# A streaming-encoder trunk in fp32: when the eighth block's weights are loaded and scaled, and in what order keys and queries are split

## The chip, the cores and the metric

The kernel runs on one core of one Trainium2 chip. The metric is the device time of a run in microseconds, the median of several runs.

## The reference

The input x has 256 rows of 2048. Layer A: RMSNorm, one projection to queries, keys, values and gate (4096 wide each, 32 heads of 128), attention with a learned bias by relative distance, product with SiLU(gate), output projection, residual. Layer B: keys and values of a shared stream, forget gates from it, queries and gate of its own projection, causal attention with accumulated decays, gate, output projection, residual. A last RMSNorm follows. Everything is float32.

```python
# layer A
q, k, v, g = split(rms_norm(x, a_norm) @ a_w_in, 4)
x = x + (chunked_relbias_attention(q, k, v, rel_bias) * silu(g)) @ a_w_out
# layer B
h_kv = rms_norm(x, kv_norm)
k, v = split(h_kv @ kv_w, 2)
cum = cumsum(log_sigmoid(h_kv @ f_w + f_b))
q, g = split(rms_norm(x, b_norm) @ b_w_in, 2)
x = x + (forgetting_attention(q, k, v, cum) * silu(g)) @ b_w_out
out = rms_norm(x, final_norm)
```

## The kernel before

Every float32 product is made of three matmuls. A factor is split into a high part (ScalarE, ACT, copies it to the rounded type fp32r) and a low part (VectorE, DVE, subtracts the high part from the original); high x high, high x low and low x high are summed by TensorE (PE), in `mm3` for the projections and `dot3` for the rest.

The heads go in 16 pairs. Each pair has two **units** of 512 weight columns: in layer A `aqk` (queries and keys) and `avg` (values and gate), in layer B `bqg` (queries and gate) and `bkv` (keys and values). A unit consumes its 2048 input rows in blocks of 256 rows; pairs after the first have seven such blocks in each unit. `Feed` brings a block in: SyncE (SP) sends the load of 512 KB into one of three raw buffers, ACT and DVE split it into one of four split buffers, PE takes 12 matmuls from it. In layer B the split also multiplies by the norm's gain. `Feed` keeps up to four blocks split ahead.

The eighth block of both units of a pair is done together in the third step of the pair's first unit, as a **quad**: its four 128-row by 512-column weight tiles (two of each unit) and four row-by-column tiles of x are multiplied in seven products instead of eight, after Strassen's scheme in Winograd's form. `Quads.products` does this from sums of x made once (`sums`) and differences of the weights. `load_quad` loads the next pair's two weight blocks into one kept buffer `raw`, in layer B scales them by the gain, and makes the first differences; `quad` splits the four operands when their turn comes in the feed. `behind` is an ordering trick: ACT copies one column of a block that is ready into the destination, so that what follows cannot be placed or sent earlier than that block's split.

The attention of a pair runs beside the projections of the following pair, as a generator (`side_a`, `side_b`, both around `attention`) that `drive` advances at the steps named in a table. Its stages: transposing queries and keys by DVE and 16 small DMAs from GpSimd (`turn`, `sums` or `b_sums` is the target), splitting keys (`wideh`, `widel`) and queries (`q1h`, `q1l`), the scores (`s1p`, `s0p`), softmax, transposing the probabilities (`sgY` to `sgZ`), splitting them (`wideh`, `widel` again), the product with the values (`op`), the gate. `B1_STEPS` says after which steps of layer B's first unit the stages of the pair before it are issued; `hooks` are calls after a step. The previous pair but one (`old`) is finished in steps 0 and 1.

The order of the program is that of issue by these tables; the tile framework's scheduler then sets the order on each engine, which runs its instructions strictly in that order. Each engine waits for others by semaphores.

Of the kernel before, what the change touches and what calls it, by code (L numbers as in the profile page):

```python
# [10 lines left out]
F32R = mybir.dt.float32r  # L11
BF16 = mybir.dt.bfloat16
AF = mybir.ActivationFunctionType
# [3 lines left out]
P = 128  # L17
S = 256
NT = S // P
# [13 lines left out]
HG = 2  # L33
NG = H // HG
GC = HG * DH
UN = 512
KB = 2
SQ = 32
# [16 lines left out]
QK7_STEPS = {0: 1, 5: 1, 6: 2}  # L55
PV7_STEPS = {0: 1}
QUAD = 7
QUAD_STEP = 3
B1_STEPS = {2: 1, 4: 1, 5: 2}
B2_STEPS = {0: 1}  # L60


def r32(ap):
    return ap.bitcast(F32)
# [3 lines left out]
def trunk(ctx, tc, x, x_t, gains, a_w_in, a_rel, a_w_out, kv_w, f_w, f_b, b_w_in, b_w_out, final_norm, out):  # L68
    nc = tc.nc
    pe, act, dve, pool, sp = nc.tensor, nc.scalar, nc.vector, nc.gpsimd, nc.sync  # L70
# [4 lines left out]
    att = ctx.enter_context(tc.tile_pool(name="att", bufs=1))  # L75
# [104 lines left out]
    class Feed:  # L180
# [68 lines left out]
                    break  # L249

        def load_quad(self, layer, g):

            q = quads[layer]
            raw, t = q.raw, q.t
            for r in range(2):
                self.behind(raw[:, r, :, :1], -1)
                sp.dma_start(out=raw[:, r], in_=q.w(r, g))
                for j in range(KB) if q.g0 else ():
                    act.activation(raw[:, r, j], raw[:, r, j], AF.Copy,  # L259
                                   scale=gain[:, q.g0[r] + QUAD * KB + j:][:, :1])  # L260
            dve.tensor_sub(t[:, 0], raw[:, 1], raw[:, :, 0])  # L261
            dve.tensor_sub(raw[:, 1, 0], raw[:, 1, 1], t[:, 0, 0])
# [66 lines left out]
    feed = Feed(todo)  # L329
# [28 lines left out]
    def rest(u):  # L358

        for b in range(u.nk // KB - u.left, u.nk // KB):  # L360
            u.step(b)
            yield u.acc
# [36 lines left out]
    def evac_scaled(acc, c0, c1, rs, dst):  # L399
        for t in range(NT):  # L400
            act.activation(dst[:, t], acc[t][:, c0:c1], AF.Copy, scale=rs[:, t:t + 1])

    def split(srcs, tag, place=None):

        n, nt = len(srcs), srcs[0].shape[1]
        hi = att.tile([P, n, nt * P], F32R, name=f"{tag}h", tag=f"{tag}h")
        lo = att.tile([P, n, nt * P], F32R, name=f"{tag}l", tag=f"{tag}l")
        if place is not None:
            feed.behind(hi[:, :, :1], place)
        for k, src in enumerate(srcs):  # L410
            h, l = (v[:, k].rearrange("p (t i u) -> p t i u", t=nt, u=SQ) for v in (hi, lo))
            act.activation(h, src, AF.Copy)
            dve.tensor_sub(l, src, r32(h))
        return hi, lo

    def dot3(out_, a, b, start=True, stop=True):
        pe.matmul(out_, a[0], b[0], start=start, stop=False)
# [3 lines left out]
    def attention(g, biases, qk, vg, half, ocat, queues=(pool,) * NQ, line=(None, None), home=None):  # L421
# [3 lines left out]
        bias1, bias0 = biases()  # L425
        qkT = z.rearrange("p i (t c) u -> p c t i u", t=NT)
        yield
        kh, kl = split([qkT[:, HG + i] for i in range(HG)], "wide", line[0])
        qh, ql = split([qkT[:, i, 1:] for i in range(HG)], "q1", line[0])
        q0 = att.tile([P, HG, P], F32, name="q0", tag="oT")  # L430
        if line[0] is not None:
            feed.behind(q0[:, :, :1], line[0])
# [48 lines left out]
        hi = ocat.hi[h0 // BIG][:, h0 % BIG:h0 % BIG + HG, :]  # L481
        lo = ocat.lo[h0 // BIG][:, h0 % BIG:h0 % BIG + HG, :]
# [15 lines left out]
    def rows(n, name):  # L498
        return att.tile([P, NT, n], F32, name=name, tag="R")
# [193 lines left out]
    rs, prev, qa = [], None, quads["a"]  # L693
    for g in range(NG):
        accs = {}
        if g:
            accs["quad"] = True
            first, second = (Unit(xT, next(order)) for _ in range(2))
            accs["qk"] = drive(rest(first), prev, PV7_STEPS,
                               {QUAD_STEP - 1: lambda: qa.products(first, second, (rsA, [(t, UN) for t in range(NT)]))})  # L700
            vg = rest(second)
        else:
            first, second = woven_units()
            rsA, halfA = rs
            accs["qk"], vg = first.acc, rest(second)
        old, prev = prev, side_a(g, accs)
        advance(prev)
        accs["vg"] = drive(vg, prev, QK7_STEPS, {0: lambda: g + 1 < NG and feed.load_quad("a", g + 1)}, old, 1)
        if not g:
            qa.sums_of_x()  # L710
        close_vg(accs)
# [150 lines left out]
    def open_b(accs):  # L862
        qk, qg = rows(UN, "qk"), accs["qg"]
        if "quad" in accs:
            qb.first_half(qk[:, :, :GC], qg, 0, rsB)
            qg = qb.whole_sums(qg, 0, GC)
        else:
            evac_scaled(qg, 0, GC, rsB, qk[:, :, :GC])
        accs["q"] = qk, gate_from(qg, GC, halfB)

    old = prev = None
    fg = forget()
    for g in range(NG):
        accs = {}
        first, second = (Unit(x1T, next(order)) for _ in range(2))
        hooks = {}
        if g:
            accs["quad"] = True
            hooks[QUAD_STEP - 1] = lambda: qb.products(first, second, (rsB, [(i, GC) for i in range(2 * NT)]))
        accs["qg"] = drive(rest(first), prev, B1_STEPS, hooks, old, 1)  # L880
        hooks = {0: lambda: g + 1 < NG and feed.load_quad("b", g + 1), 2: lambda: open_b(accs)}
        accs["kv"] = drive(rest(second), prev if g else fg, B2_STEPS if g else {1: 1, 2: 1, 4: 1, 6: 1}, hooks)
        if not g:
            qb.sums_of_x()
        old, prev = prev, side_b(g, accs)
        advance(prev)
# [95 lines left out]
```

## Time and profile before

| | |
|---|---|
| runs | 1879.86, 1882.55, 1884.58 us; median 1882.55 |
| profiled execution | 1873.8 us, of it a span of 1872.1 |
| mean granted clock of TensorE | 0.994 |
| DMA | 396.37 MB, mean 212 GB/s |

The profile is of one execution, and it was a faster one than the three timed. In its rows L232 is line 232 of the kernel, PE is TensorE's matmuls and PEld its weight loads, an arrow `out<-in` names the tiles. Layer A's pairs run from about 11 to 705 us, its output projection to 915, layer B's pairs from there to 1651, its output projection to the end.

### The profile page before, as it was taken

To read this page: it belongs to the slowest core of one execution; us is meant where nothing else is said; L and a number is where in the kernel's file an instruction comes from. 1 tells how busy PE (TensorE), PEld (TensorE's weight loads), DVE (VectorE), ACT (ScalarE), POOL (GpSimd) and SP (SyncE) were. 2 spreads that over 40 slices of the span, in tenths; PEclk is the share of its full clock that TensorE was granted. 3 is DMA by queue.
4 is the path that set the end of the run, shared out by engine and by line. 5 is a ranking of instruction groups with operands and counts; after the bars stand their busy time and mean duration, and the time that the engine had idled before them with its cause. 6 is when DMAs were issued, how large, how long until landed. Compare 5 with 4: busy or idle time off the path is not lost.

```text
span 1872.1 us, 25978 instructions
## 1 busy us (share of the span) xinstructions
PE 1840.7 (98%) x8297; PEld 1514.4 (81%) x8297; DVE 1424.1 (76%) x2094; ACT 1184.7 (63%) x2233; POOL 522.2 (28%) x1071
## 2 busy tenths in 40 slices
PE   9999999999999999999999999999999999999998
PEld 7888888888888888888887878878778887878886
DVE  7877878888788877555678878888888878886554
ACT  6665656666566656444567777777777777775443
POOL 1222222232222223221023333333323333333000
PEclk9999999999999999999999999999999999999999
DMA  8666666666666666776656656666666665667664
GB/s 283 214 212 212 225 215 220 213 219 213 210 213 213 210 210 207 240 234 224 209 176 204 206 198 211 210 208 210 208 207 202 216 204 194 210 220 222 206 202 158
DMA packets 143144, 396.37 MB, mean 212 GB/s; under 512 B 31104, under 2 KB 37536, under 8 KB 142880
## 3 DMA queue, kind: packets, MB, share of 16 engines
q1 hardware_dynamic: 106960, 354.25, 57.7%
q0 software_dynamic: 32256, 37.29, 6.7%
q10 hardware_dynamic: 3792, 3.17, 0.6%
q8 instruction: 66, 1.08, 0.2%
q14 instruction: 70, 0.57, 0.1%
HBM read 351.05 MB, written 4.23 MB: 190 GB/s over the span
## 4 chain that ended last, share of the span: by engine, by line
PE 30%; DMA 12%; DVE 10%; ACT 9%; issue 3%; POOL 0%; ACTq 0%; DVEq 0%
PE bo_acc L176 9%; PE ao_acc L176 8%; PE bqg_acc L176 5%; DMA b_quad<-in_kv_w 5%; DMA bqg_raw<-in_b_w_in 3%; DVE bqg_lo L233 3%; PE bkv_acc L176 3%; DMA bkv_raw<-in_kv_w 3%; ACT bkv_hi L232 3%; ACT sg L451 1%; DVE bkv_lo L233 1%; PE avg_acc L176 1%; PE aqk_acc L176 1%; ACT b_quad L259 1%; DVE b_quad L261 1%
## 5 line engine op out<-in xcount | busy, mean ns | idle before, releaser
L395 POOL DMA_DIRECT2D sgZ<-sgY x512 | 251.4, 498 | 529.2 <-PE bkv_acc L176 299.9
L236 ACT ACTIVATE avg_hi<-avg_raw 128x1024 fp32r<-128x1024 f32 x112 | 118.7, 1060 | 138.3 <-DMA avg_raw<-in_a_w_in 76.7
L237 DVE TENSOR_TENSOR avg_lo<-avg_raw,avg_hi 128x1024 fp32r<-128x1024 f32 x112 | 136.2, 1217 | 87.8 <-ACT avg_hi L236 87.6
L232 ACT ACTIVATE bqg_hi<-bqg_raw,gain 128x512 fp32r<-128x512 f32 x226 | 150.1, 713 | 60.3 <-DMA bqg_raw<-in_b_w_in 49.0
L233 DVE SCALAR_TENSOR_TENSOR bqg_lo<-bqg_raw,gain,bqg_hi 128x512 fp32r<-128x512 f32 x226 | 163.6, 773 | 26.5 <-ACT bqg_hi L232 26.3
L233 DVE SCALAR_TENSOR_TENSOR bkv_lo<-bkv_raw,gain,bkv_hi 128x512 fp32r<-128x512 f32 x226 | 159.0, 744 | 22.8 <-ACT bkv_hi L232 22.6
L176 PE MATMUL bqg_acc<-bqg_hi,x1Th 128*128 128x512 f32 x452 | 174.7, 398 | 0.0
L176 PE MATMUL bqg_acc<-bqg_lo,x1Th 128*128 128x512 f32 x452 | 174.4, 397 | 0.0
L176 PE MATMUL bqg_acc<-bqg_hi,x1Tl 128*128 128x512 f32 x452 | 173.1, 394 | 0.0
L176 PE MATMUL aqk_acc<-aqk_hi,xTh 128*128 128x512 f32 x452 | 173.0, 394 | 0.0
L176 PE MATMUL avg_acc<-avg_hi,xTh 128*128 128x512 f32 x452 | 172.3, 393 | 0.0
L176 PE MATMUL aqk_acc<-aqk_lo,xTh 128*128 128x512 f32 x452 | 170.9, 390 | 0.4 <-DVE aqk_lo L237 0.4
L176 PE MATMUL aqk_acc<-aqk_hi,xTl 128*128 128x512 f32 x452 | 171.0, 390 | 0.0
L176 PE MATMUL avg_acc<-avg_hi,xTl 128*128 128x512 f32 x452 | 170.9, 390 | 0.0
L176 PE MATMUL bkv_acc<-bkv_hi,x1Th 128*128 128x512 f32 x452 | 170.8, 389 | 0.0
L176 PE MATMUL bkv_acc<-bkv_lo,x1Th 128*128 128x512 f32 x452 | 170.8, 389 | 0.0
L176 PE MATMUL bkv_acc<-bkv_hi,x1Tl 128*128 128x512 f32 x452 | 170.7, 389 | 0.0
L176 PE MATMUL avg_acc<-avg_lo,xTh 128*128 128x512 f32 x452 | 170.6, 389 | 0.0
L395 POOL DMA_DIRECT2D b_sums<-b_quad x256 | 125.8, 499 | 151.2 <-issue 86.6
L232 ACT ACTIVATE bkv_hi<-bkv_raw,gain 128x512 fp32r<-128x512 f32 x226 | 150.4, 712 | 18.1 <-DMA bkv_raw<-in_kv_w 7.5
L395 POOL DMA_DIRECT2D sums<-quad x192 | 94.7, 499 | 219.4 <-PE op L475 84.5
L237 DVE TENSOR_TENSOR aqk_lo<-aqk_raw,aqk_hi 128x1024 fp32r<-128x1024 f32 x110 | 132.2, 1221 | 26.6 <-ACT aqk_hi L236 25.8
(317 smaller groups left out, 4372.9 us busy)
## 6 DMA issues: line engine op xcount, KB each, us to landing
bqg_raw<-in_b_w_in SPq DMA_DIRECT2D x113, 512.0 KB, 4.3
bkv_raw<-in_kv_w SPq DMA_DIRECT2D x113, 512.0 KB, 3.6
avg_raw<-in_a_w_in SPq DMA_DIRECT2D x112, 512.0 KB, 4.7
aqk_raw<-in_a_w_in SPq DMA_DIRECT2D x110, 512.0 KB, 4.1
ao_raw<-in_a_w_out SPq DMA_DIRECT2D x64, 512.0 KB, 4.2
bo_raw<-in_b_w_out SPq DMA_DIRECT2D x64, 512.0 KB, 4.2
sgZ<-sgY POOLq DMA_DIRECT2D x512, 40.0 KB, 4.4
quad<-in_a_w_in SPq DMA_DIRECT2D x32, 512.0 KB, 5.8
```

The source lines that it names most:

```text
L176: pe.matmul(acc[t], x[:, t * P:(t + 1) * P], w, start=t not in begun, stop=k == nk - 1 and i == 2)
L232: act.activation(hi[:, j], raw[:, j], AF.Copy, scale=gk)
L233: dve.scalar_tensor_tensor(lo[:, j], raw[:, j], gk, r32(hi[:, j]), op0=OP.mult, op1=OP.subtract)
L236: act.activation(hi[:, j], raw[:, j], AF.Copy)
L237: dve.tensor_sub(lo[:, j], raw[:, j], r32(hi[:, j]))
L259: act.activation(raw[:, r, j], raw[:, r, j], AF.Copy, scale=gain[:, q.g0[r] + QUAD * KB + j:][:, :1])
L261: dve.tensor_sub(t[:, 0], raw[:, 1], raw[:, :, 0])
L395: queues[j].dma_start(out=r32(z)[j * SQ:(j + 1) * SQ, i], in_=y[i * SQ:(i + 1) * SQ, j])
L451: act.activation(s_[:, i], s_[:, i], AF.Exp, bias=nm[:, t, i:i + 1], accum_out=sm[:, t, i:i + 1])
```

## The change

It has three parts.

1. `load_quad` is cut in two. The loads stay in it and are now called after step 5 of a pair's first unit (`LOAD_STEP`) in both layers; before, all of it was called after step 0 of the second unit. (In layer A's first pair they are called between the units.)
2. The scalings (layer B alone) and the first differences become `differ`. Layer A calls it after step 0 of the second unit, as before; layer B after step 3.
3. `split_pairs` splits several groups together, head by head: keys of head 0, queries of head 0, keys of head 1, queries of head 1, instead of both heads' keys and then both heads' queries. In layer B the stage is issued one step sooner (`B1_STEPS`: 3 in place of 4).

```diff
-B1_STEPS = {2: 1, 4: 1, 5: 2}
+LOAD_STEP = 5
+B1_STEPS = {2: 1, 3: 1, 5: 2}
...
         def load_quad(self, layer, g):
+            q = quads[layer]
+            for r in range(2):
+                self.behind(q.raw[:, r, :, :1], -1)
+                sp.dma_start(out=q.raw[:, r], in_=q.w(r, g))
+
+        def differ(self, layer):
             q = quads[layer]
             raw, t = q.raw, q.t
             for r in range(2):
-                self.behind(raw[:, r, :, :1], -1)
-                sp.dma_start(out=raw[:, r], in_=q.w(r, g))
                 for j in range(KB) if q.g0 else ():
                     act.activation(raw[:, r, j], raw[:, r, j], AF.Copy,
                                    scale=gain[:, q.g0[r] + QUAD * KB + j:][:, :1])
...
+    def split_pairs(many, place=None):
+        out = []
+        for srcs, tag in many:
+            nt = srcs[0].shape[1]
+            out.append([att.tile([P, len(srcs), nt * P], F32R, name=f"{tag}{x}", tag=f"{tag}{x}") for x in "hl"])
+            if place is not None:
+                feed.behind(out[-1][0][:, :, :1], place)
+        for k in range(len(many[0][0])):
+            for (srcs, _), (hi, lo) in zip(many, out):
+                h, l = (v[:, k].rearrange("p (t i u) -> p t i u", t=srcs[k].shape[1], u=SQ) for v in (hi, lo))
+                act.activation(h, srcs[k], AF.Copy)
+                dve.tensor_sub(l, srcs[k], r32(h))
+        return out
...
-        kh, kl = split([qkT[:, HG + i] for i in range(HG)], "wide", line[0])
-        qh, ql = split([qkT[:, i, 1:] for i in range(HG)], "q1", line[0])
+        (kh, kl), (qh, ql) = split_pairs([([qkT[:, HG + i] for i in range(HG)], "wide"),
+                                          ([qkT[:, i, 1:] for i in range(HG)], "q1")], line[0])
...
             accs["qk"] = drive(rest(first), prev, PV7_STEPS,
-                               {QUAD_STEP - 1: lambda: qa.products(...)})
+                               {QUAD_STEP - 1: lambda: qa.products(...),
+                                LOAD_STEP: lambda: g + 1 < NG and feed.load_quad("a", g + 1)})
...
-        accs["vg"] = drive(vg, prev, QK7_STEPS, {0: lambda: g + 1 < NG and feed.load_quad("a", g + 1)}, old, 1)
+        accs["vg"] = drive(vg, prev, QK7_STEPS, {0: lambda: g + 1 < NG and feed.differ("a")}, old, 1)
...
+        hooks[LOAD_STEP] = lambda: more and feed.load_quad("b", g + 1)
         accs["qg"] = drive(rest(first), prev, B1_STEPS, hooks, old, 1)
-        hooks = {0: lambda: g + 1 < NG and feed.load_quad("b", g + 1), 2: lambda: open_b(accs)}
+        hooks = {2: lambda: open_b(accs), 3: lambda: more and feed.differ("b")}
```

What the scheduler makes of it in layer B, in one pair. In the names below `bqg_hi`, `bkv_hi` are split blocks, `b_quad_8492` the quad's raw buffer, `b_quad_8493` its differences, `b_comb` the quad products' sums. First place, the second unit: the loads on SP's queue, from the third `kv` load on. Before:

```order
L197 DMA bkv_raw_13408<-in_kv_w 128x1024
L197 DMA bkv_raw_13428<-in_kv_w 128x1024
L197 DMA bkv_raw_13465<-in_kv_w 128x1024
L834 DMA cb<-cumd 128x512
L197 DMA bkv_raw_13506<-in_kv_w 128x1024
L197 DMA bkv_raw_13526<-in_kv_w 128x1024
L257 DMA b_quad_8492<-in_b_w_in 128x1024
L257 DMA b_quad_8492<-in_kv_w 128x1024
L197 DMA bqg_raw_13582<-in_b_w_in 128x1024
```

After:

```order
L198 DMA bkv_raw_13408<-in_kv_w 128x1024
L198 DMA bkv_raw_13445<-in_kv_w 128x1024
L198 DMA bkv_raw_13465<-in_kv_w 128x1024
L256 DMA b_quad_8492<-in_b_w_in 128x1024
L256 DMA b_quad_8492<-in_kv_w 128x1024
L198 DMA bkv_raw_13510<-in_kv_w 128x1024
L198 DMA bkv_raw_13530<-in_kv_w 128x1024
L846 DMA cb<-cumd 128x512
L198 DMA bqg_raw_13576<-in_b_w_in 128x1024
```

The two quad loads moved from behind the seventh `kv` load to behind the fifth; the load of the decays `cb` moved from behind the fifth to behind the seventh.

Then ACT at the same place: the ordering copies of the quad loads (`b_quad_8492<-bkv_hi`), the scalings and the last `kv` blocks. Before, from the gate's scaling to the gate of the next pair:

```order
L462 ACTIVATE sg<-gs,csc 128x128 x4
L280 ACTIVATE b_quad_8492<-bkv_hi_13520 128x2 x2
L232 ACTIVATE bkv_hi_13576<-bkv_raw_13465,gain 128x512 x2
L841 ACTIVATE d_13729<-cb,cum 128x128
L232 ACTIVATE bkv_hi_13596<-bkv_raw_13506,gain 128x512 x2
L842 ACTIVATE cb<-cb,cum 128x256
L841 ACTIVATE d_13729<-cb,cum 128x128
L842 ACTIVATE cb<-cb,cum 128x256
L232 ACTIVATE bkv_hi_13626<-bkv_raw_13526,gain 128x512
L259 ACTIVATE b_quad_8492<-b_quad_8492,gain 128x512 x4
L505 ACTIVATE gs<-b_comb,half_b 128x256 x2
```

After, from the third `kv` block on:

```order
L233 ACTIVATE bkv_hi_13504<-bkv_raw_13408,gain 128x512
L285 ACTIVATE b_quad_8492<-bkv_hi_13459 128x2 x2
L233 ACTIVATE bkv_hi_13504<-bkv_raw_13408,gain 128x512
L461 ACTIVATE sg,sm<-sg,nm 128x256 x2
L461 ACTIVATE sg,sm<-sg,nm 128x128 x2
L233 ACTIVATE bkv_hi_13524<-bkv_raw_13445,gain 128x512 x2
L472 ACTIVATE sg<-gs,csc 128x128 x4
L233 ACTIVATE bkv_hi_13570<-bkv_raw_13465,gain 128x512 x2
L264 ACTIVATE b_quad_8492<-b_quad_8492,gain 128x512 x2
L233 ACTIVATE bkv_hi_13590<-bkv_raw_13510,gain 128x512 x2
L264 ACTIVATE b_quad_8492<-b_quad_8492,gain 128x512 x2
L233 ACTIVATE bkv_hi_13620<-bkv_raw_13530,gain 128x512
```

The copies moved ahead of the softmax (`sg`), and the four scalings, which stood together behind the first half of the last block, stand two and two ahead of it; the four decays' instructions (`d`, `cb`) moved behind the last `kv` block, past the end of these rows.

Second place, ACT at the split of keys and queries. Before:

```order
L232 ACTIVATE bkv_hi_13422<-bkv_raw_13374,gain 128x512 x2
L627 ACTIVATE b_comb<-b_comb,rstd_b 128x256 x2
L280 ACTIVATE wideh<-bkv_hi_13422 128x2
L280 ACTIVATE q1h<-bkv_hi_13422 128x2
L280 ACTIVATE q_13456<-bkv_hi_13422 128x2
L412 ACTIVATE wideh<-b_sums 128x256 x2
L412 ACTIVATE q1h<-b_sums 128x128 x2
L433 ACTIVATE q_13456<-b_sums 128x256
L232 ACTIVATE bkv_hi_13459<-bkv_raw_13385,gain 128x512 x2
```

After:

```order
L233 ACTIVATE bkv_hi_13439<-bkv_raw_13374,gain 128x512
L285 ACTIVATE wideh<-bqg_hi_13402 128x2
L637 ACTIVATE b_comb<-b_comb,rstd_b 128x256 x2
L285 ACTIVATE q1h<-bqg_hi_13402 128x2
L419 ACTIVATE wideh<-b_sums 128x256
L419 ACTIVATE q1h<-b_sums 128x128
L419 ACTIVATE wideh<-b_sums 128x256
L419 ACTIVATE q1h<-b_sums 128x128
L285 ACTIVATE q_13436<-bqg_hi_13402 128x2
L233 ACTIVATE bkv_hi_13439<-bkv_raw_13374,gain 128x512
L443 ACTIVATE q_13436<-b_sums 128x256
```

The split moved ahead of the second half of the first `kv` block, keys and queries alternate, and the ordering copies read a `qg` block.

Third place, DVE at the end of a pair, from the first `qg` blocks of the next pair to the transposition of queries and keys. Before:

```order
L233 SCALAR_TENSOR_TENSOR bqg_lo_13647<-bqg_raw_13582,gain,bqg_hi_13646 128x512 x2
L233 SCALAR_TENSOR_TENSOR bqg_lo_13667<-bqg_raw_13602,gain,bqg_hi_13666 128x512 x2
L632 SCALAR_TENSOR_TENSOR qk<-bkv_acc_13262,rstd_b,b_comb 128x256
L233 SCALAR_TENSOR_TENSOR bqg_lo_13687<-bqg_raw_13632,gain,bqg_hi_13686 128x512 x2
L632 SCALAR_TENSOR_TENSOR qk<-bkv_acc_13263,rstd_b,b_comb 128x256
L638 TENSOR_TENSOR b_comb<-bkv_acc_13262,b_comb 128x256
L638 TENSOR_TENSOR b_comb<-bkv_acc_13263,b_comb 128x256
L392 STREAM_TRANSPOSE b_quad_8493<-qk 128x1024
```

After:

```order
L234 SCALAR_TENSOR_TENSOR bqg_lo_13647<-bqg_raw_13576,gain,bqg_hi_13646 128x512
L234 SCALAR_TENSOR_TENSOR bqg_lo_13667<-bqg_raw_13596,gain,bqg_hi_13666 128x512 x2
L234 SCALAR_TENSOR_TENSOR bqg_lo_13687<-bqg_raw_13626,gain,bqg_hi_13686 128x512 x2
L642 SCALAR_TENSOR_TENSOR qk<-bkv_acc_13262,rstd_b,b_comb 128x256
L648 TENSOR_TENSOR b_comb<-bkv_acc_13262,b_comb 128x256
L642 SCALAR_TENSOR_TENSOR qk<-bkv_acc_13263,rstd_b,b_comb 128x256
L648 TENSOR_TENSOR b_comb<-bkv_acc_13263,b_comb 128x256
L397 STREAM_TRANSPOSE b_quad_8493<-qk 128x1024
```

The third `qg` block's low half (`bqg_lo_13687`) moved ahead of the first sum for the keys (`qk`).

More of the change, by code (lines that the diff above doesn't have):

```diff
@@ L401, in evac_scaled @@
             act.activation(dst[:, t], acc[t][:, c0:c1], AF.Copy, scale=rs[:, t:t + 1])
-    def split(srcs, tag, place=None):
[L405 to L414, printed above, removed]
+    def split_pairs(many, place=None):
[11 more added lines that the diff above has]
+        return out
+    def split(srcs, tag, place=None):
+        return split_pairs([(srcs, tag)], place)[0]
     def dot3(out_, a, b, start=True, stop=True):
@@ L699, in trunk @@
             accs["qk"] = drive(rest(first), prev, PV7_STEPS,
-                               {QUAD_STEP - 1: lambda: qa.products(first, second, (rsA, [(t, UN) for t in range(NT)]))})
+                               {QUAD_STEP - 1: lambda: qa.products(first, second, (rsA, [(t, UN) for t in range(NT)])),
+                                LOAD_STEP: lambda: g + 1 < NG and feed.load_quad("a", g + 1)})
             vg = rest(second)
@@ L705, in trunk @@
             accs["qk"], vg = first.acc, rest(second)
+            feed.load_quad("a", 1)
         old, prev = prev, side_a(g, accs)
         advance(prev)
-        accs["vg"] = drive(vg, prev, QK7_STEPS, {0: lambda: g + 1 < NG and feed.load_quad("a", g + 1)}, old, 1)
+        accs["vg"] = drive(vg, prev, QK7_STEPS, {0: lambda: g + 1 < NG and feed.differ("a")}, old, 1)
         if not g:
@@ L879, in trunk @@
             hooks[QUAD_STEP - 1] = lambda: qb.products(first, second, (rsB, [(i, GC) for i in range(2 * NT)]))
+        more = g + 1 < NG
+        hooks[LOAD_STEP] = lambda: more and feed.load_quad("b", g + 1)
         accs["qg"] = drive(rest(first), prev, B1_STEPS, hooks, old, 1)
-        hooks = {0: lambda: g + 1 < NG and feed.load_quad("b", g + 1), 2: lambda: open_b(accs)}
+        hooks = {2: lambda: open_b(accs), 3: lambda: more and feed.differ("b")}
         accs["kv"] = drive(rest(second), prev if g else fg, B2_STEPS if g else {1: 1, 2: 1, 4: 1, 6: 1}, hooks)
```

## The prediction

> **What bounds the kernel now.** I read the page's busy shares first, then the matmul engine's time per head pair, then who waits for whom, and last the chain of waits through one bad pair.
>
> ```profile
> span 1872.1 us, 25978 instructions
> PE 1840.7 (98%) x8297; PEld 1514.4 (81%) x8297; DVE 1424.1 (76%) x2094; ACT 1184.7 (63%) x2233; POOL 522.2 (28%) x1071
> ```
>
> PE has a record open 98% of the span. The change removes no matmul, so a gain can only be time in which PE waits or runs slowly. The table of stretches shows where that is. Columns: stretch, its length, busy time with instruction counts of PE, PEld, DVE, ACT and POOL, granted PE clock, DMA share, GB/s.
>
> ```profile
> 99.60:693.90 594.30, 592.39 (x2721) 492.03 (x2719) 479.77 (x638) 364.72 (x664) 181.35 (x377) 1.00 0.67 215
> 236.80:282.00 45.20, 45.20 (x211) 37.75 (x211) 35.37 (x48) 27.55 (x52) 13.97 (x29) 1.00 0.67 211
> 1010.30:1637.40 627.10, 610.98 (x2719) 498.74 (x2717) 525.76 (x874) 465.93 (x975) 219.76 (x442) 0.99 0.63 205
> 1446.50:1493.20 46.70, 46.40 (x211) 37.87 (x210) 40.70 (x68) 36.12 (x76) 16.96 (x34) 1.00 0.66 214
> 1346.70:1396.60 49.90, 47.79 (x210) 39.25 (x209) 41.99 (x70) 35.80 (x75) 16.57 (x35) 0.97 0.63 207
> 1299.90:1313.50 13.60, 13.42 (x62) 10.78 (x61) 11.58 (x20) 9.56 (x16) 6.39 (x13) 1.00 0.42 133
> 1346.70:1363.20 16.50, 14.61 (x63) 12.15 (x62) 13.30 (x22) 9.54 (x16) 7.95 (x17) 0.90 0.47 153
> ```
>
> Rows one and three are thirteen pairs of layer A and thirteen of layer B: the same matmuls (2721 and 2719 records), 594.3 us against 627.1. A pair of A without a gap takes 45.2 us (row two); B's mean is 627.1 / 13 = 48.2. B's pairs differ among themselves, the best at 46.7 us and a bad one at 49.9, and the last two rows show that good and bad part in the stretch from a pair's first matmul to its quad products: 13.6 against 16.5 us for the same work, the bad one at a clock of 0.90.
>
> The waits of PE in layer B, 1010 to 1651 us (waiter, line, what it waits for: total us, times, longest):
>
> ```profile
> PE op L418 <- DVE widel L413: 13.6, 11, 2.4
> PE s1p L417 <- ACT q1h L412: 1.8, 4, 0.7
> ```
>
> The first is the probabilities' product, waiting for DVE's low halves of the probabilities. Why DVE is late there is read in the chain of waits through the pair that ends at 1346.7 (start, length, what):
>
> ```profile
> 1332.17 8.19 DMA b_quad<-in_kv_w
> 1340.38 1.34 ACT b_quad L259 x2
> 1341.75 1.23 DVE b_quad L261
> 1344.25 0.67 DVE bkv_lo L233
> 1344.94 3.42 DMA bqg_raw<-in_b_w_in
> 1348.44 0.73 ACT bqg_hi L232
> 1349.20 1.41 DVE bqg_lo L233 x2
> 1351.59 1.23 DVE b_quad L392
> 1352.82 1.10 DVE quad_lo L273
> 1353.92 0.35 DVE widel L413
> 1354.32 0.51 PE op L418
> ```
>
> The quad's second load takes 8.19 us. ACT reaches its scaling first and stands still; DVE's differences stand behind it; behind them stands the split of the last `kv` block, whose raw buffer the third `qg` block's load needs. That load therefore goes out only at 1344.94, its split comes at 1348.44, and everything DVE does for the next pair is pushed back until PE stands at `op`. In the rows of ACT and of DVE (in brackets: idle time before, and what ended it) stand the splits of the second and third `kv` block, the ordering copies of the quad loads, the split of the sixth `kv` block, the two waits, and for comparison the third `qg` block at the start of the good pair:
>
> ```profile
> 1323.64 2.55 ACT L232 ACTIVATE bkv_hi<-bkv_raw,gain 128x512 fp32r<-128x512 f32 x4
> 1331.53 0.28 ACT L280 ACTIVATE b_quad<-bkv_hi 128x2 f32<-128x2 f32 x2
> 1333.31 1.34 ACT L232 ACTIVATE bkv_hi<-bkv_raw,gain 128x512 fp32r<-128x512 f32 x2
> 1340.38 1.34 ACT L259 ACTIVATE b_quad<-b_quad,gain 128x512 f32<-128x512 f32 x2 [2.40 <-DMA b_quad<-in_kv_w]
> 1341.75 1.23 DVE L261 TENSOR_TENSOR b_quad<-b_quad 128x1024 f32<-128x1024 f32 x1 [3.85 <-ACT b_quad L259]
> 1299.84 1.34 ACT L232 ACTIVATE bqg_hi<-bqg_raw,gain 128x512 fp32r<-128x512 f32 x2 [2.75 <-DMA bqg_raw<-in_b_w_in]
> ```
>
> Even in the good pair that block's load is late. Only its start differs: 1299.84 is 0.1 us before its pair's first matmul, 1348.44 is 1.7 us after.
>
> A bad pair loses more than the wait. After 1.89 us of it PE's rows are twice as far apart for a while:
>
> ```profile
> 1354.32 0.51 PE L418 MATMUL op<-widel,vh 128*128 128x256 f32 x1 [1.89 <-DVE widel L413]
> 1357.18 0.63 PE L176 MATMUL bqg_acc<-bqg_hi,x1Tl 128*128 128x512 f32 x1
> 1357.61 0.51 PE L176 MATMUL bqg_acc<-bqg_hi,x1Th 128*128 128x512 f32 x1
> 1358.43 0.39 PE L176 MATMUL bqg_acc<-bqg_hi,x1Th 128*128 128x512 f32 x1
> 1358.66 0.39 PE L176 MATMUL bqg_acc<-bqg_lo,x1Th 128*128 128x512 f32 x1
> ```
>
> From 1357.18 to 1357.61 is 0.43 us, later 0.23. A clock of 0.90 over 16.5 us is 1.65 us lost, so wait and clock together make most of the 2.9 us between the two stretches. I take the slow clock to follow from the wait and to go with it. The Trainium skill ("TensorE: Matmul & The Clock Gate", the part on the clock gate) says that the clock is halved only after an idle window of about 3.4 us. This trace differs: 1.89 us was followed by the doubled spacing. By the page's rule the slow clock would have another cause and stay, and the gain below would shrink by five bad pairs at 1.65 us, or 8 us; the measurement decides.
>
> **The change part by part.** Nothing is added or removed on PE, ACT or DVE: each pair still has two loads, two ordering copies, four scalings and two differences. So the work itself costs 0; places count.
>
> *Quad loads, layer B.* They go out behind the fifth `kv` load and ahead of the sixth, where they stood behind the seventh. ACT's ordering copies move from behind the gate scalings (1331.5 in the shown pair) to the third `kv` block, about 1326, so the loads start some 6 us earlier. Even at 8.19 us they land at about 1334; the scalings now stand two and two, the last behind the sixth block's split, which ended at 1334.6 before. ACT's wait of 2.40 and DVE's 3.85 go. What is late next: the third `qg` load needs the seventh `kv` block's split, which then waits only for PE to free a split buffer. It should start 2 to 4 us sooner, as DVE's stall was 3.85.
>
> Bounds of what this is worth. If every pair becomes the best of B, 13 x (48.2 - 46.7) = 20 us. If B's pair becomes A's, 13 x (48.2 - 45.2) = 39 us; that includes the split of keys and queries below. The best pair still has the third `qg` block on its chain, 2.75 us late, and if that goes too the chain to `widel` gets shorter than PE's need. I therefore take the pair start nearer to A's level: of the 1.5 us between 46.7 and 45.2 about 0.5 belongs to the next edit, and of the other 1.0 I take 0.7, over 14 pair starts 10 us. Sum of this edit: 30.
>
> One order on DVE speaks against it: the third `qg` split now stands ahead of the first `qk` sum. If that block were still late, one sum of 0.5 us more would stand behind it.
>
> *Keys and queries, head by head, one step sooner.* In the next pair:
>
> ```profile
> 1369.81 1.34 ACT bkv_hi L232 x2
> 1372.44 0.40 ACT wideh L412
> 1372.84 0.40 ACT q1h L412 x2
> 1373.10 0.39 PE L417 MATMUL s1p<-wideh,q1h 128*128 128x256 f32 x1 [0.22 <-ACT q1h L412]
> ```
>
> The scores wait for a split that stands behind a whole `kv` block. Now half of that block (1.34 / 2 = 0.67 us) moves behind the split, and the first head's queries come ahead of the second head's keys (another 0.3). PE's wait of 0.22 and the slower matmuls behind it, some 0.5 us a pair, are covered. Bounds 0 and 0.8 us; I take 0.35 x 15 = 5 us. The split still waits behind half a block whose load bounds it, hence not all.
>
> *The rest, at 0.* The load of `cb` moves behind two `kv` loads, its four readers on ACT behind the last `kv` split; the scores that need them are a pair's first unit away. GpSimd keeps its order. In layer A the loads start about one block earlier and the differences stay; A's thirteen pairs are 594.3 - 13 x 45.2 = 6.7 us above the undisturbed one, so the bounds are +3 (two more disturbed pairs) and -6. I take 0.
>
> The sum: 30 + 5 = 35 us. Against the profiled execution's own 1873.8 us (span 1872.1 and 1.7 around it) that is 1838.8. The median of the runs, 1882.55, stands 8.75 above that execution; I subtract from the median: 1847.5.
>
> **The rivals.** *A: only the bad pairs get better.* The third `qg` load may be bounded by its own issue, not by the quads; the 2.75 us in a good pair speaks for it. Then 20 us: 1862.5.
>
> *B: the wait only moves.* The quads go ahead of the sixth and seventh `kv` blocks, ACT stands as long for those, and the third `qg` block is as late as now: 1882. Against it: the loads no longer meet the `qg` loads that were sent at 1334 while the second quad load was under way.
>
> *C, slower: the sixth `kv` block comes too late.* Loads of one queue:
>
> ```profile
> bkv_raw<-in_kv_w SPq DMA_DIRECT2D x113, 512.0 KB, 3.6
> b_quad<-in_kv_w SPq DMA_DIRECT2D x15, 512.0 KB, 6.5
> ```
>
> PE needs the sixth block 24 matmuls before the pair's end, 5.5 us before 1346.7; two halves on ACT and DVE take 1.34 and 1.41, so it must land by about 1338.4. If quads from 1326 take 8.19 us and the block another 3.6 behind them, it lands at 1337.9: 0.5 us of room. Beyond that every pair starts like the bad ones: 13 x (49.9 - 48.2) = 22 us more, 1904. The Trainium skill ("DMA: Bandwidth & Descriptors", queues, rings and completion order) says that descriptors are taken in the order of the ring, which would put the block wholly behind the quads; the trace agrees so far as the second quad load's 6.5 us exceed a single load's 3.6. Against C: 8.19 was with two `qg` loads and the probabilities' transposition beside it, and at 1326 there is little else.
>
> **How the numbers follow.** Forecast 0.55, A 0.20, B 0.12, C 0.13. A change under 0.3% (5.6 us) can't be told from none. Forecast and A are faster, with a little of B: 0.77; same 0.11; slower 0.12. Low end: the 39 us and the 8.75 us that the profiled execution already lacked, with layer A's 2 to 3 us, give 1832. High end: halfway from A to B, 1872, which leaves B and C out.
>
> **What would show it.** In layer B: ACT's and DVE's waits at the quad scalings gone; `op` waiting for `widel` under 3 us in all instead of 13.6; no stretch with a clock under 0.99; pairs of about 45.8 us. The scores' waits under 1 us. Wrong if ACT's waits for the raw `kv` blocks grow past 30 us (B, C), or if the third `qg` block still starts after the pair's first matmul (A).

## The result and the profile after

| | median of the runs, us | lowest to highest | ratio to before, 95% interval |
|---|---|---|---|
| before, same chip | 1881.20 (4 runs) | 1879.05 to 1884.58 | |
| after | 1837.86 (4 runs) | 1834.56 to 1838.27 | 0.9764 [0.9744, 0.9784] |
| after, on a second chip (before there: 1876.91) | 1833.68 (4 runs) | 1829.29 to 1835.31 | 0.9776 [0.9750, 0.9802] |

The change saves 43 us, 2.3%. The forecast was 1847.5. The profiled execution took 1838.27 us. First its page: the span, and each engine's busy time, share and instructions.

```profile
span 1836.6 us, 26020 instructions
PE 1819.0 (99%) x8297; PEld 1509.0 (82%) x8297; DVE 1429.2 (78%) x2094; ACT 1187.8 (65%) x2233; POOL 522.5 (28%) x1071
```

The number of matmuls is the same, 8297, and so are the counts on DVE, ACT and POOL. PE's busy time fell all the same, from 1840.7 to 1819.0 us, so part of the time that was lost in before had counted as busy. The table of stretches says where (columns as in the prediction): thirteen pairs of layer A, thirteen of layer B, then two pair starts in B, from the first matmul to the quad products.

```profile
98.20:687.90 589.70, 589.32 (x2719) 491.69 (x2718) 481.38 (x638) 367.42 (x664) 180.56 (x377) 1.00 0.67 217
1006.30:1600.70 594.40, 592.80 (x2719) 492.70 (x2718) 527.72 (x873) 465.27 (x975) 221.20 (x442) 1.00 0.66 216
1280.10:1292.90 12.80, 12.80 (x63) 10.77 (x62) 10.35 (x18) 8.45 (x14) 7.30 (x15) 1.00 0.33 102
1188.60:1202.10 13.50, 13.19 (x63) 10.84 (x62) 11.94 (x20) 8.87 (x15) 7.84 (x16) 1.00 0.43 133
```

Layer B's pairs went from 627.1 to 594.4 us, 32.7 of the 35.5 by which the span fell. Length less PE's busy time is PE's gaps: 627.10 - 610.98 = 16.1 us before, 594.40 - 592.80 = 1.6 after, so 14.5 us were waits that show as gaps. Busy time itself fell by 610.98 - 592.80 = 18.2 us with equal counts. Of that the slower clock is less than half: the granted clock was at half in five stretches of 3.41 us in these pairs before, and in none after, which is 5 x 3.41 / 2 = 8.5 us at most (an estimate). The rest is short waits. The ends of matmuls are modelled, so a short wait hides behind the modelled end of the matmul before it; it shows at the weight loads (PEld), first before, then after, over 960 to 1650 us:

```profile
PEld op L418 <- DVE widel L413: 23.2, 27, 2.6
PEld op L428 <- DVE widel L420: 2.0, 5, 0.5
```

So some 24 of the 32.7 us were waits and some 8 the clock. A pair start now takes 12.8 us (row three), less than the 13.6 of before's good pair; in ten of the fourteen starts it is 12.77, and three are at 13.5 to 13.7 like row four.

The waits of PE in layer B, 960 to 1650 us:

```profile
PE s1p L427 <- ACT q1h L419: 1.7, 1, 1.7
PE op L428 <- DVE widel L420: 0.9, 3, 0.3
```

The wait at `op` was 13.6 us in 11 and is 0.9 in 3. The one wait of 1.7 us at the scores stands in the sixteenth and last pair, outside the thirteen of the table (the 10 us after it, from 1624.8, ran at a clock of 0.83). The pairs do not end where the section on the profile before put it: by the matmuls' rows of before, layer A's run to 739 us and layer B's to 1685. On ACT and on DVE over the same time (waiter, what it waits for: total us, times, longest):

```profile
ACT bqg_hi L233 <- DMA bqg_raw<-in_b_w_in: 15.5, 18, 2.8
ACT bkv_hi L233 <- DMA bkv_raw<-in_kv_w: 13.6, 23, 1.2
ACT bqg_hi L233 <- PE bkv_acc L177: 3.3, 3, 1.3
```

No row for the quads' scalings is left, on ACT or on DVE. What these two had shown before:

```profile
ACT bqg_hi L232 <- DMA bqg_raw<-in_b_w_in: 47.3, 21, 4.5
ACT bkv_hi L232 <- DMA bkv_raw<-in_kv_w: 5.9, 11, 1.0
ACT b_quad L259 <- DMA b_quad<-in_kv_w: 11.3, 13, 2.4
DVE b_quad L261 <- ACT b_quad L259: 33.7, 14, 3.9
```

ACT's 11.3 us at the scalings and DVE's 33.7 behind them are gone, ACT waits 32 us less for raw `qg` blocks, and 8 us more for raw `kv` blocks, which now stand behind the quad loads. The pair that starts at 1280.1 shows the order that does it, in ACT's and then DVE's rows (in brackets: idle time before, and what ended it):

```profile
1266.56 1.32 ACT L264 ACTIVATE b_quad<-b_quad,gain 128x512 f32<-128x512 f32 x2
1267.78 1.33 ACT L233 ACTIVATE bkv_hi<-bkv_raw,gain 128x512 fp32r<-128x512 f32 x2
1269.01 1.32 ACT L264 ACTIVATE b_quad<-b_quad,gain 128x512 f32<-128x512 f32 x2
1277.67 1.34 ACT L233 ACTIVATE bqg_hi<-bqg_raw,gain 128x512 fp32r<-128x512 f32 x2 [1.33 <-PE bkv_acc L177]
1283.46 0.42 DVE L420 TENSOR_TENSOR widel<-sgZ,wideh 128x256 fp32r<-128x256 f32 x1
```

The scalings wait for nothing. The third `qg` block, at 1348.44 in the bad pair and 1.7 us behind its pair's first matmul, is split at 1277.67, 2.5 us ahead of it, and waits not for its load but for PE to free a split buffer. `widel` is there at 1283.88, nearly 2 us before PE comes to `op`. The chain of waits from 1268 to 1290 us is now PE alone until the third step (start, length, what):

```profile
1267.88 12.47 PE bkv_acc L177 x55
1280.35 5.44 PE bqg_acc L177 x24
1285.79 0.12 PE op L427
```

### The profile page after: what moved, and what is told of

The parts are those of the page before. It is cut to its first block, busy times and chain, and to the rows that moved or that the text cites. A ratio compares the mean times of both kernels' runs of the same rounds, so it can differ in the third digit from the quotient of the medians.

```text
span 1836.6 us, 26020 instructions
## 1 busy us (share of the span) xinstructions
PE 1819.0 (99%) x8297; PEld 1509.0 (82%) x8297; DVE 1429.2 (78%) x2094; ACT 1187.8 (65%) x2233; POOL 522.5 (28%) x1071
## 4 chain that ended last, share of the span: by engine, by line
PE 52%; DMA 4%; DVE 4%; ACT 3%; issue 2%; POOL 0%; ACTq 0%; DVEq 0%
PE bkv_acc L177 13%; PE bqg_acc L177 12%; PE bo_acc L177 9%; PE ao_acc L177 8%; DMA bkv_raw<-in_kv_w 2%; PE avg_acc L177 2%; PE aqk_acc L177 2%; DVE bqg_lo L234 2%; DMA bqg_raw<-in_b_w_in 1%; DVE bkv_lo L234 1%; DMA xinZ<-xinY 1%; PE s0p L451 1%; PE op L485 1%; ACT quad_hi L277 0%; PE p L428 0%
## 5 line engine op out<-in xcount | busy, mean ns | idle before, releaser
L233 ACT ACTIVATE bqg_hi<-bqg_raw,gain 128x512 fp32r<-128x512 f32 x226 | 150.4, 713 | 30.9 <-DMA bqg_raw<-in_b_w_in 18.7
L233 ACT ACTIVATE bkv_hi<-bkv_raw,gain 128x512 fp32r<-128x512 f32 x226 | 152.6, 712 | 17.5 <-DMA bkv_raw<-in_kv_w 13.6
```

Of the source, the lines that this page charges most:

```text
L233: act.activation(hi[:, j], raw[:, j], AF.Copy, scale=gk)
```

## The experiments

In the table "B" is the length of the stretch of layer B's thirteen pairs in the profiled execution; "starts" is what the fourteen pair starts there take beyond the matmuls' undisturbed spacing, "rest" the same for the remainder of the thirteen pairs, both summed from the starts of the matmuls in the trace.

| kernel | median us | lowest to highest | ratio, 95% | B | starts | rest |
|---|---|---|---|---|---|---|
| before | 1881.20 | 1879.05 to 1884.58 | | 627.1 | 36.7 | 13.5 |
| before again | 1876.78 (1 run) | | | 631.3 | 38.9 | 16.0 |
| after | 1837.86 | 1834.56 to 1838.27 | 0.9764 [0.9744, 0.9784] | 594.4 | 8.1 | 8.2 |
| quads alone | 1842.33 | 1838.40 to 1848.45 | 0.9815 [0.9765, 0.9865] | 597.6 | 5.5 | 14.0 |
| split alone | 1885.39 | 1877.48 to 1901.74 | 1.0066 [1.0030, 1.0102] | 636.8 | 48.8 | 11.0 |
| early loads, scalings at step 0 | 1860.40 | 1852.66 to 1866.91 | 0.9914 [0.9882, 0.9946] | 618.1 | 33.3 | 8.7 |
| late loads, scalings at step 3 | 1849.76 | 1847.11 to 1855.43 | 0.9862 [0.9805, 0.9918] | 604.0 | 19.4 | 7.9 |
| layer A put back | 1836.26 | 1829.98 to 1839.05 | 0.9802 [0.9773, 0.9831] | 590.3 | 5.8 | 6.5 |
| step alone, with the quads | 1842.39 | 1840.09 to 1845.27 | 0.9837 [0.9807, 0.9868] | 602.3 | 5.5 | 18.7 |
| heads alone, with the quads | 1837.68 | 1834.17 to 1839.34 | 0.9810 [0.9780, 0.9840] | 598.1 | 6.7 | 13.4 |
| scalings at step 4 | 1833.51 | 1829.84 to 1836.60 | 0.9788 [0.9758, 0.9819] | 591.7 | 6.6 | 6.9 |
| after again | 1833.68 | 1829.29 to 1835.31 | 0.9776 [0.9750, 0.9802] | 591.8 | 6.3 | 7.5 |
| scalings at step 4 again | 1832.62 | 1831.56 to 1835.63 | 0.9778 [0.9753, 0.9803] | 591.7 | 7.2 | 6.4 |

Each ratio is to runs of the kernel before on the same chip, whose medians were 1877.03, 1876.47 and 1876.91 us for the rows from the fourth, the eighth and the twelfth on.

**The quads alone.** From the kernel after:

```diff
-B1_STEPS = {2: 1, 3: 1, 5: 2}
+B1_STEPS = {2: 1, 4: 1, 5: 2}
-        (kh, kl), (qh, ql) = split_pairs([...keys...], [...queries...])
+        kh, kl = split([...keys...], "wide", line[0])
+        qh, ql = split([...queries...], "q1", line[0])
```

> The quads' loads, scalings and differences as in the changed kernel, the split of keys and queries as before (both keys, then both queries; stage issued after step 4). Theory: the quads carry nearly all, the split some 5 us: 1843 us (1840 to 1847), with the wait of op for widel as short as in the changed kernel and the scores' waits of before back, 0.3 to 0.5 us a pair. Rival: the split carries a third or more of the 43 us, since a late split also delays the kv blocks behind it: 1852 or more.

**The split alone.** From the kernel before, only the split of keys and queries and its step are those of after.

> The quads as in the kernel before in both layers, the split of keys and queries as in the changed kernel. Theory: 1876 us (1872 to 1880): the waits of ACT and DVE at the quad scalings (10.6 and 30 us in layer B) and op's wait for widel (13.6 us) stay. Rival (the split carries a third): under 1867 us and op's wait under 8 us.

Measured: the quads alone give 1842.33, as the theory had it, 35 us below before; all fourteen pair starts are at 12.77 us, and only the scores wait:

```profile
PE s1p L427 <- ACT q1h L419: 5.1, 8, 1.8
```

The split alone is slower than before by 0.66% [0.30, 1.02], where some gain was expected. Its waits of PE in layer B, and the ACT rows around one pair's start:

```profile
PE op L441 <- DVE widel L433: 23.7, 14, 2.4
PE bkv_acc L177 <- DVE bkv_lo L234: 2.9, 4, 1.0
1255.53 1.34 ACT L277 ACTIVATE b_quad<-b_quad,gain 128x512 f32<-128x512 f32 x2 [1.18 <-DMA b_quad<-in_kv_w]
1265.20 1.34 ACT L233 ACTIVATE bqg_hi<-bqg_raw,gain 128x512 fp32r<-128x512 f32 x2 [4.14 <-DMA bqg_raw<-in_b_w_in]
```

It did at the scores what it was expected to do (rest 11.0 against 13.5), but the wait at `op` grew from 13.6 to 23.7 us. That PE comes sooner to the pair's end and waits there for a chain that comes no sooner can explain only the 2.5 us that it gained in the rest, not the 12.1 lost at the starts. The clock is not the reason either: it fell five times in these pairs, as in the first profile of before. The trace shows that the chain itself was later. On the mean of the fourteen starts the last `kv` split on DVE ended 2.4 us ahead of the pair's first matmul (3.25 and 2.98 in the two profiles of before), and the split of the third `qg` block began 1.7 us behind it (0.8 and 1.1). Why the chain is later stays open. So the two parts do not add: the split costs 8 us by the medians (12 by the ratio) without the quads' part and saves 4.5 to 8.6 with it (1842.33 less the two medians of after; the three come from three chips, and by the ratios, whose intervals overlap, it is 7 to 10).

**Early loads, but the scalings at once.** From the kernel after:

```diff
-        hooks = {2: lambda: open_b(accs), 3: lambda: more and feed.differ("b")}
+        hooks = {0: lambda: more and feed.differ("b"), 2: lambda: open_b(accs)}
```

> The changed kernel, with layer B's scalings and differences after step 0 of the second unit, as early as before, and the loads early. Theory (what cost was ACT standing at a load that had not landed): the scalings now stand ahead of the fifth kv block and wait for loads that land about 14 us ahead of the pair's end, 1 to 2.5 us of wait per pair on ACT, but with three more kv blocks to go, which PE's buffers cover: 1840 us (1836 to 1848). Rival (the loads' meeting with the qg loads was what cost, the place of the scalings nothing): equal to the changed kernel within 2 us.

**Late loads, with the scalings after step 3.** From the kernel after:

```diff
-        hooks[LOAD_STEP] = lambda: more and feed.load_quad("b", g + 1)
-        hooks = {2: lambda: open_b(accs), 3: lambda: more and feed.differ("b")}
+        hooks = {0: lambda: more and feed.load_quad("b", g + 1), 2: lambda: open_b(accs), 3: lambda: more and feed.differ("b")}
```

> The changed kernel, with layer B's quad loads sent after step 0 of the second unit, as late as before; scalings and differences after step 3, which puts all four behind the last kv split. Theory (the wait at the scalings was the cost): ACT's wait for the quad load falls under 3 us in all, the last kv split no longer stands behind it, 1845 us (1838 to 1855). Rival (the cost is that the quad loads and the qg loads share the queue): the third qg block starts as late as before and op waits 8 us or more in all, 1862 us or more.

Measured: early loads with early scalings gave 1860.40, and neither theory had that: they keep 17 us of a gain of 43. Late loads with late scalings gave 1849.76, within what the theory said. So the place of the scalings is worth more (1860.4 against 1833.7 to 1837.9: 23 to 27 us) than the place of the loads (1849.8 against the same: 12 to 16). The medians are from different chips; by the ratios to before it is 26 to 28 us against 16 to 18. Why, ACT's and DVE's rows of the first of the two show:

```profile
1280.71 2.69 ACT L264 ACTIVATE b_quad<-b_quad,gain 128x512 f32<-128x512 f32 x4
1283.30 2.55 ACT L233 ACTIVATE bkv_hi<-bkv_raw,gain 128x512 fp32r<-128x512 f32 x4
1286.16 1.33 ACT L233 ACTIVATE bkv_hi<-bkv_raw,gain 128x512 fp32r<-128x512 f32 x2
1289.64 0.89 DVE L234 SCALAR_TENSOR_TENSOR bkv_lo<-bkv_raw,gain,bkv_hi 128x512 fp32r<-128x512 f32 x1
1295.20 1.34 ACT L233 ACTIVATE bqg_hi<-bqg_raw,gain 128x512 fp32r<-128x512 f32 x2 [0.19 <-DMA bqg_raw<-in_b_w_in]
1301.00 0.42 DVE L420 TENSOR_TENSOR widel<-sgZ,wideh 128x256 fp32r<-128x256 f32 x1
```

No scaling waits here: the four run in one piece, 2.69 us. But they stand ahead of the last three `kv` blocks, the last `kv` split on DVE ends at 1290.5, and the raw buffers go to the `qg` loads late. The third `qg` block is at 1295.20, as late as in the kernel before (its pair's first matmul is at 1295.1), and ACT waits for the loads as much as there:

```profile
ACT bqg_hi L233 <- DMA bqg_raw<-in_b_w_in: 50.1, 42, 2.5
PE op L428 <- DVE widel L420: 16.9, 27, 2.4
```

In the kernel with late loads the same two waits are 24.7 and 7.2 us. So the time at which the last `kv` split frees its raw buffer counts: a wait for the quads' load ahead of it delays it, and so does the quads' own work of 2.7 us on ACT and 1.9 on DVE. It is not all that counts. With late loads the third `qg` load goes out as early as in the kernel after (on the mean of the fourteen starts 6.5 and 6.2 us ahead of the pair's first matmul), but the quads' loads were sent just ahead of the `qg` loads, and the first three of these take 6.9, 7.6 and 5.5 us to land where they take 4.8, 5.0 and 4.2 there. The third block's split begins 0.9 us ahead of the first matmul in place of 1.9. The rival of late loads, the shared queue, has that part.

**Layer A put back.** Its loads and differences are issued together after step 0 of the second unit, as before; the rest is after.

> Only layer A is put back: its quad loads and differences are issued together after step 0 of the second unit, as before; layer B and the split of keys and queries are as in the kernel after. Layer A's thirteen pairs took 594.3 us before and 589.7 after. Theory 1: the earlier loads made that difference, so the thirteen pairs take 594 us again, the first pair's end is later too (about 1 us), and the median is some 5 us above the kernel after: 1843. Theory 2 (the prediction's term of 0): the 4.6 us are the split head by head or chance, and this kernel equals the kernel after within 2 us. In both, layer B's thirteen pairs stay at 594.4 within 2 us.

Measured: 1836.26 us, between the two medians of the kernel after. Theory 1's 1843 fails. In its profile the thirteen pairs of layer A take 592.2 us, and those of layer B 590.3, outside the 2 us that both theories had allowed there. Layer A's stretch was 592.0 us in the second profile of before and 588.3 in that of after. In the seven profiles whose layer A is that of after it ran from 588.3 to 591.6 us, so single executions of it differ by some 3 us, and the 4.6 us between the first two profiles are at most partly the change's.

**Step alone, and heads alone.** Both from the kernel after; the first keeps both heads' keys ahead of both heads' queries (the second edit of the quads alone), the other issues the stage at step 4 (its first edit).

> The quads as in the kernel after, and the split of layer B's keys and queries a step sooner, but both heads' keys first and then both heads' queries, in both layers. With the quads alone the median was 1842.3 and the waits and slow matmuls in the rest of layer B's pairs came to 14.0 us against 8.2 after. Theory: the step carries it, since the half kv block of 0.67 us that stood ahead of the split is more than the 0.3 us by which the first head's queries come sooner; 1839 (1837 to 1841), the rest of the pairs at 9 to 11 us. Rival: the order of the heads carries it; 1842, the rest at 13 to 14.

> The quads as in the kernel after, keys and queries split head by head in both layers, but layer B's stage issued at step 4 as before. Theory: the step carries most of what the split brings, so this stays near the kernel with the quads alone: 1841 (1839 to 1843), the scores' wait for q1h back at 3 to 5 us in layer B. Rival: the order of the heads carries it; 1838, the scores' wait under 2 us.

Measured: 1842.39 for the step alone, as if nothing had been added to the quads; 1837.68 for the order of the heads. The rival was right on the first as to the time, though the rest, 18.7 us, is above what both had (9 to 14). The step alone brings the scores forward into a new wait, for the low half of the queries, at each of the fourteen pairs:

```profile
PE s1p L429 <- DVE q1l L420: 4.0, 14, 0.3
PE s1p L427 <- ACT q1h L419: 2.5, 7, 0.7
```

For the heads alone the rival's time and wait came too (1837.68, and 0.9 us at the scores in two waits), but times and profile do not agree: by the times it is near the kernel after and below the step alone in every run, by its one profile layer B is as with the quads alone (598.1 against 597.6, rest 13.4 against 14.0), and it was layer A, 588.3 us, that was short in that execution. In the profiles only both edits together bring the rest down to about 8. How the 5 us divide stays open.

**Scalings a step later still.** From the kernel after, `differ` of layer B after step 4 in place of 3; and once more beside the kernel after on one chip.

> Early loads as in the kernel after, but layer B's scalings and differences are called a step later still, after step 4 of the second unit, so that all four scalings stand behind the sixth kv block's split or later. With late loads and this kind of place the median was 1849.8, with early loads and scalings ahead of the last three blocks 1860.4. Theory (what counts is that no kv split stands behind the quads): the third qg load goes out as early as after or up to 1 us earlier, the three pair starts of 13.5 to 13.7 us come down to 12.8, and the time is 1836 (1833 to 1839). Rival: the quads' own operands now come late for the next pair's third step, or the four scalings stand ahead of the first qg splits; the pair starts rise above 13.5 and the time is 1842 or more.

> Layer B's scalings and differences after step 4 instead of 3, once more beside the kernel after: on different chips the medians were 1833.5 and 1837.9. Theory: no kv split stands behind the quads any more, worth the 2 us of the three imperfect pair starts, so it is 1 to 5 us below the kernel after on the same chip. Rival: the difference was the chip's, and the two agree within 1 us.

> The kernel after, unchanged, on the chip of the next one, so that the two are compared directly and on another chip than the first: 1837 us (1833 to 1840).

Measured: 1833.51, and side by side 1832.62 against 1833.68, with ratios of 0.9778 and 0.9776 whose intervals lie on each other. The rival holds: the chip or the execution made the difference. Starts of 13.5 us come and go in both kernels (after again has none over 13.1). Neither is shown better, and no experiment beats the kernel after by more than can be told from nothing.

**The kernel before, profiled again.**

> The kernel before, unchanged, profiled a second time: its executions ran from 1863 to 1888 us, while those of the kernel after ran from 1834.6 to 1838.3. Theory: the spread is the number and depth of bad pair starts in layer B, so of this profile's difference from the first one's 1873.8 us two thirds or more lies in the stretches from a pair's first matmul to its quad products (36.7 us above the undisturbed length in all there), and the rest of the pairs stays at 13.5 within 3 us. Rival: the spread lies anywhere (layer A, the output projections), and the pair starts stay at 36.7 within 3 us.

Measured: 1876.78 us, 3.0 above the first profile. Layer B's pairs took 4.2 us more (starts 2.2 more, rest 2.5), layer A's 2.3 less. By their letter both theories came true (2.2 is over two thirds of 3.0 and the rest moved by less than 3; 38.9 is within 3 of 36.7), so a difference so small does not decide. That executions of before range from 1863 to 1888 us goes in part with the mean clock recorded with each: of 38 executions the two at 0.999 took 1863.48 and 1864.49 us, the one at 0.992 took 1887.63. Seven thousandths of 1870 us are 13 us, about half of that range; the other half is not explained. Executions of the kernel after lie within 9 us on two chips.

## Why the prediction was right, point by point

**The quads in layer B, 30 us.** The chain was the right one, and the signs asked for came: no wait at the scalings, 0.9 us at `op` where under 3 was asked, pairs of 594.4 / 13 = 45.7 us where 45.8 was, and no clock under 0.99 in any of the thirteen pairs. The scores' wait, asked under 1 us, was 1.7, once, in the last pair. The quads alone measured 1842.33 against 1877.03, 34.7 us, so by the medians the term was some 5 too small; by layer B's stretches in the profiles, 627.1 and 597.6, it is 29.5 and right. It had taken 0.7 of the 1.0 us between B's best pair and A's; the pair starts came down wholly, to 12.77 us in all fourteen. One reason stood in the prediction and was half wrong: it put the gain on the waits of ACT (2.40) and DVE (3.85) for the second load. With the waits gone and the scalings still ahead of the `kv` splits, only 17 of 43 us came. The place of the scalings, two and two between the last three `kv` splits, was given no price of its own, and it is the larger part: 23 to 27 us where undone, against 12 to 16 for the loads.

**The split, 5 us.** With the quads' part in place it is 4.5 to 8.6 (1842.3 less 1837.9 or 1833.7). The step that failed is that it was costed as a term that adds by itself, bounded by 0 below: alone it costs 8.4 us (1885.39 - 1877.03). Why it costs there is open. And its working, that half a `kv` block less ahead of the split covers PE's wait, did not hold for the step by itself, which turned the wait for `q1h` into one for `q1l`.

**Layer A and the rest, 0.** The profile showed -4.6, within the bounds of +3 and -6; with layer A put back the median does not rise. 0 was as good a value as the runs can show.

**The sum.** 35 us stood against 35.5 between the two profiled spans, but 43 between medians, on both chips. The prediction saw that the profiled execution of before lay 8.75 us below the median and then subtracted a sum drawn from that execution. The second profiles of both kernels show the same: 1876.78 less 1829.29 is 47.5 us, of it 631.3 - 591.8 = 39.5 in layer B's pairs. So the sum was right for the execution that it was drawn from and some 8 us short for the median: a worse execution of before has more to lose, while after, which waits little, hardly varies. In part the match is luck: of the 35.5 us, 32.7 lie in layer B, where all 35 were forecast, 4.6 in layer A, where 0 was, and the remainder of the span took 1.8 more. Where in before the difference between executions lies is shown only for the clock's share of it.

**The worry about DVE's order** (the third `qg` split ahead of the first `qk` sum) cost nothing that shows: the block came 0.6 to 2.5 us ahead of its pair's first matmul in the pairs of layer B.

**The rivals.** A fell: the third `qg` load was not bounded by its own issue, and starts below B's best of before were reached. B and C showed their sign, ACT's waits for raw `kv` blocks at 13.6 us against 5.9, far from the 30 that would have decided. C's room of 0.5 us (0.6 by its own terms, 1338.4 less 1326 + 8.19 + 3.6) was never used up: the longest of these waits is 1.2 us and PE has none at `kv`.

**The clock.** The slow clock went with the waits, as taken: five stretches at half clock in the thirteen pairs before, none after. By the Trainium skill's rule of an idle window of about 3.4 us ("TensorE: Matmul & The Clock Gate", the part on the clock gate) it would have stayed and cost 8 us. One reading of the working was off: 1.89 us of wait and 1.65 of clock are not "most of" the 2.9 us between the bad start and the good one but more, 3.5. The good start had short waits of its own, 13.6 us where 12.8 was reached.

## What to carry to other kernels

When a late load holds up an engine, follow which buffer is freed late because of it, and keep other work, even work that waits for nothing, from standing in one piece ahead of the split that frees that buffer, and other loads from being sent just ahead of the late one; loading earlier alone gave less than half here. A saving in front of a bound chain need not be a small gain: here it was a loss of 8 us by itself and a gain with the other part, so test such parts alone and together. A sum drawn from one profiled execution is compared with that execution; where executions of the kernel before scatter and the change takes away what scatters, the median gains more.

## What the runs showed of the hardware

The traces record the granted clock. It falls to half for stretches of 3.41 us (and for one of 6 to 9 us at the very end of each run). In layer B's pairs of the kernel before these begin at 1115.49, 1258.86, 1354.43, 1405.63 and 1548.99 us: 42, 28, 15 and 42 times 3.413 us apart. In every other trace with more than one such stretch their starts, too, are whole multiples of 3.413 us apart, as if on a grid.

A wait's length does not by itself say whether the clock falls after it. In the kernel with the split alone two waits at `op` were of 2.22 and 2.38 us, and the 6 us behind them (from 1220.8 and from 1418.4) had these rows:

```profile
1220.83 0.39 PE L441 MATMUL op<-widel,vh 128*128 128x256 f32 x1 [2.22 <-DVE widel L433]
1418.36 0.38 PE L441 MATMUL op<-widel,vh 128*128 128x256 f32 x1 [2.38 <-DVE widel L433]
1220.80:1226.80 6.00, 5.89 (x21) 4.68 (x22) 4.40 (x8) 1.65 (x3) 6.00 (x14) 0.72 0.24 67
1418.40:1424.40 6.00, 5.92 (x29) 4.75 (x30) 4.65 (x9) 3.06 (x5) 6.00 (x14) 1.00 0.24 68
```

After the shorter wait the clock was 0.72 and 21 matmuls ran, after the longer one 1.00 and 29. Cut along the grid, the rows around the two waits tell them apart (the columns are those of the table of stretches: PE's busy time comes first behind the length, the clock is the third number from the end):

```profile
1219.05:1222.46 3.41, 1.55 (x8) 1.14 (x9) 3.41 (x6) 1.00 (x3) 2.59 (x6) 1.00 0.36 131
1222.46:1225.88 3.42, 3.42 (x11) 2.80 (x10) 2.74 (x6) 1.38 (x3) 3.42 (x8) 0.50 0.25 70
1413.61:1417.02 3.41, 2.25 (x10) 1.39 (x8) 3.41 (x7) 3.27 (x7) 0.00 (x0) 1.00 0.39 129
1417.02:1420.44 3.42, 1.99 (x11) 1.57 (x12) 3.36 (x5) 0.81 (x2) 3.03 (x7) 1.00 0.25 86
1420.44:1423.85 3.41, 3.41 (x16) 2.78 (x16) 2.35 (x5) 2.00 (x3) 3.41 (x8) 1.00 0.24 67
```

The shorter wait lies almost whole in one interval: PE is idle for 3.41 - 1.55 = 1.86 us of it, and the next interval runs at 0.50. The longer one lies across 1417.02 and leaves 1.16 and 1.43 us of idle time to two intervals, and the clock stays. Counted over all thirteen traces, each of the 16 intervals with 1.7 us or more of idle time was followed by one at half clock; of the 29 with 1.07 to 1.61 us seven were, and what decides among those is not shown. So where the grid falls on a wait can make one execution of a kernel slower than another; that this is the clock's share of the scatter of before is argued, not tested.
